# TensorE's instruction order in the token mixers written by hand, and the delta rule's forward substitution moved from VectorE to GpSimd

## The chip, the cores and the metric

The kernel runs on one core of one Trainium2 chip. The metric is device time in microseconds (us) of one execution, lower is better. In the profile the core's engines are PE (TensorE, matrix products), PEld (its weight loads, which overlap PE), DVE (VectorE), ACT (ScalarE), POOL (GpSimd) and SP (SyncE, which issues most transfers).

## The reference, cut to what matters

Two layers over 256 tokens of width 1024. Each layer is a gated feed-forward half step and a layer norm, three token mixers on the same input with gates and one output projection, a norm, a second feed-forward half step and a norm. The change is in the mixers.

```python
def hybrid_layer(x, mem_n, ...):
    h = layer_norm(DEEPNORM_ALPHA * x + 0.5 * swiglu(x, ffn1_w_gu, ffn1_w_down), ln_g[0], ln_b[0])
    (dn_q, dn_k, dn_v, dn_b, dn_a, dn_z, sw_q, sw_k, sw_v, xa_q, gates) = jnp.split(h @ w_in, split_idx, axis=-1)
    o_dn = deltanet_branch(dn_q, dn_k, dn_v, dn_b, dn_a, dn_z, dn_conv_w, ...)
    o_sw = sliding_window_attention(sw_q, sw_k, sw_v, swa_sinks)
    o_xa = memory_cross_attention(xa_q, mem_n, w_mem_kv)
    branches = jnp.stack([o_dn, o_sw, o_xa], axis=2)
    gates = jax.nn.sigmoid(gates.reshape(B_, S_, N_BRANCH, D))
    merged = jnp.sum(gates * jnp.einsum('bsnc,ncd->bsnd', branches, w_branch), axis=2)
    h = layer_norm(DEEPNORM_ALPHA * h + merged @ w_out, ln_g[1], ln_b[1])
    return layer_norm(DEEPNORM_ALPHA * h + 0.5 * swiglu(h, ffn2_w_gu, ffn2_w_down), ln_g[2], ln_b[2])
```

In the DeltaNet branch, keys, queries and values pass a causal convolution of four taps, and each chunk needs a unit triangular system solved:

```python
    a = jnp.where(strict, jnp.einsum('bhncd,bhnsd->bhncs', k_beta, k) * decay, 0.0)
    t_mat = a + jnp.eye(C, dtype=f32)
    sol = lax.linalg.triangular_solve(t_mat, rhs, left_side=True, lower=True, unit_diagonal=True)
```

## The kernel before, in words

**Products.** Every large matrix product takes fp32 operands split into a high and a low part and is done as three passes (high by high, high by low, low by high). Weights come in units of 128x1024 fp32 (512 KB). For each, SP issues the transfer into `raw`, ACT casts the high part (`whi`, L116), DVE subtracts it to leave the low part (`wlo`, L117), and PE multiplies. `projB` (L135 to L137) makes transposed results 256 wide, `projA` with `mm3` (L121 to L123) makes rows of 512. PSUM has three pools: `acc` with four buffers, `at` with two (attention) and `sm` with two (small steps).

**Stages of the mixers.** They take 222 to 482 us of the span in the first layer and 886 to 1149 in the second. First come the projections of z, the gate inputs and the sliding window's values, then three convolutions (k, q, v), the cross-attention's queries (`xq`) and the window's keys and queries (`sq_`). Beside them the DeltaNet is prepared: `tok` turns k, v and q, the decay g is made by a chain of short DVE steps, and the products of keys with keys and queries, times the decay, end up in `AK` (L534 and L535 on PE, L538 on DVE).

**The inverse.** Each triangular system, of 128 rows here, is inverted in blocks. The 16x16 diagonal blocks are gathered by a mask and a sum (L543, L544), written to DRAM on POOL's queue (L546, tile `dr`) and read back spread over 128 partitions (L550, tiles `w2` and `w3`). Fifteen steps of substitution follow, each a product (L576) and a sum (L577) on DVE, 128 partitions by 8x15 elements at first and 8x1 at the end. L581 widens the result to blocks of 32, L583 transposes it, and small products on PE (L597 to L643) double the blocks to 64 and 128, with copies on ACT and POOL between.

**The rest.** The cross-attention (L690 to L713) makes scores, a softmax on DVE and ACT, transposes of the probabilities on PE (L708) and values (L713); the sliding window does the same (L734 to L758). For each branch, gates of 16 units and a branch projection of four units follow, then the output projection.

**What sets the order.** A scheduler orders each engine's queue by the program's order and priorities. Weight transfers and splits get a higher priority. PE's order in the mixers is the scheduler's as well; the program lists all the DeltaNet, then both attentions, then the gates, and the scheduler fills gaps of one with matrix work of another. Each engine runs its queue in order, so an instruction that waits holds up all behind it. Two places restrict it: `together` keeps four small PE instructions adjacent, and the substitution is issued after the last query split:

```python
with tc.issue_after(last_q):
    for j in range(15):
        n = 15 - j
        nc.vector.tensor_tensor(pr16[:, :, 0:n], ab[j // 8][:, j % 8, :, j + 1:16], ...)
        nc.vector.tensor_tensor(y16[:, :, j + 1:16], y16[:, :, j + 1:16], pr16[:, :, 0:n], op=ALU.add)
```

Of the kernel before, what the change touches and what calls it, by code (L numbers as in the profile page):

```python
# [38 lines left out]
def tile_trunk(ctx, tc, x, xT, mem, wst, lnp, memln, cvw, rows, cst, out):  # L39
# [78 lines left out]

    def mm3(o, l, r, first, last, skip=False):
        (lh, ll), (rh, rl) = l, r  # L120
        nc.tensor.matmul(o, lh, rh, start=first, stop=False, skip_group_check=skip)  # L121
        nc.tensor.matmul(o, lh, rl, start=False, stop=False, skip_group_check=skip)  # L122
        nc.tensor.matmul(o, ll, rh, start=False, stop=last, skip_group_check=skip)  # L123

    def projB(xt, nt, kpu, behind=None):
        banks = [acc().rearrange("p (t s) -> p t s", t=2) for _ in range((nt + 1) // 2)]
        for uu in range(KD // kpu):
            hi, lo = unit(behind=behind)
            for kk in range(kpu):
                k = uu * kpu + kk  # L130
                for t in range(nt):
                    c = (kk * nt + t) * P
                    o = banks[t // 2][:, t % 2, :]
                    lastt = t % 2 == 1 or t == nt - 1
                    nc.tensor.matmul(o, hi[:, c:c + P], xt[0](k), start=(k == 0 and t % 2 == 0), stop=False, skip_group_check=True)  # L135
                    nc.tensor.matmul(o, hi[:, c:c + P], xt[1](k), start=False, stop=False, skip_group_check=True)  # L136
                    nc.tensor.matmul(o, lo[:, c:c + P], xt[0](k), start=False, stop=(k == KD - 1 and lastt), skip_group_check=True)  # L137
        return banks

    def projA(xt, w, kpu, nk, outs, tail=0, dsts=(), lead=0, after=None, behind=None, held=()):  # L140
# [23 lines left out]
        for tb in range(2):  # L164
            run(range(lead), tb, range(len(outs[tb])))
        for uu in range(lead, nu - tail):
            for tb in range(2):
                run([uu], tb, range(len(outs[tb])))
# [28 lines left out]
    def to_T(put, tb, src, q):  # L197

        ps = sm()
        for j in range(4):  # L200
            k = q * 4 + j
            nc.tensor.transpose(ps[:, j * P:(j + 1) * P], src[:, k * P:(k + 1) * P], ident)  # L202
# [193 lines left out]
    def mixers(l, hT, mkT, mv_, post):  # L396
        xt = acc_of(hT)

# [17 lines left out]
        def conv(seg, dst):  # L416
            for i, b in enumerate(projB(xt, 4, 2)):
# [7 lines left out]
                silu[:] = [nc.scalar.activation(dst[:, 2 * i:2 * i + 2, :], yc, AF.Silu).ins]  # L425

        kT = T(pu, [P, 4, S], "u0")
        conv(1, kT)
        qT = T(pu, [P, 4, S], "u1")
        conv(0, qT)  # L430
        vT = T(pu, [P, 4, S], "u8")
        conv(2, vT)

        ssq = T(pu, [P, 2, 2, 4], "ssq")
        ktok = T(pu, [P, 4, P], "u9")
        vin = T(pu, [P, 2, 4, P], "u2")

        def tok(src, tb):
            ps = sm()
            for h in range(4):  # L440
                nc.tensor.transpose(ps[:, h * P:(h + 1) * P], src[:, h, tb * P:(tb + 1) * P], ident)
# [7 lines left out]
        for tb in range(2):  # L449
            ps = tok(kT, tb)  # L450
            sumsq(ps, ssq[:, 0, tb, :])
            if tb == 0:
                nc.scalar.copy(ktok, ps)
        nc.vector.tensor_scalar(ssq[:, 0], ssq[:, 0], RMS_EPS, None, ALU.add)
        rk2 = T(pu, [P, 2, 4], "rk2")
        nc.vector.reciprocal(rk2, ssq[:, 0])
        kn = T(pu, [P, 2, 4], "kn")
        rsqrt(kn, ssq[:, 0], T(pu, [P, 2, 4], "knt"))
        nc.vector.tensor_tensor(kn, ssq[:, 0], kn, op=ALU.mult)
        for tb in range(2):  # L460
            ps = tok(vT, tb)
            nc.vector.tensor_tensor(vin[:, tb], ps, kn[:, tb, :].unsqueeze(2).to_broadcast([P, 4, P]), op=ALU.mult)
        for tb in range(2):
            sumsq(tok(qT, tb), ssq[:, 1, tb, :])
        qeps = T(pu, [P, 2, 4], "qeps")
        nc.vector.tensor_scalar(qeps, ssq[:, 1], RMS_EPS, RMS_EPS * P, ALU.add, ALU.mult)
# [38 lines left out]
        ps = sm()  # L505
        gf = g.rearrange("p t h -> p (t h)")
        nc.tensor.matmul(ps[:, 0:8], tri, gf, start=True, stop=True)
        nc.tensor.matmul(ps[:, 8:16], mlt, gf, start=True, stop=True)
        eg = T(pu, [P, 2, 2, 4], "eg")
        nc.scalar.activation(eg.rearrange("p a t h -> p (a t h)"), ps[:, 0:16], AF.Exp)  # L510
        ks = T(pu, [P, 4], "ks")
        nc.vector.tensor_tensor(ks, cS[:, 0, :], eg[:, 1, 0, :], op=ALU.mult)
        neg1 = T(pu, [P, 4], "neg1")
        nc.vector.tensor_scalar(neg1, eg[:, 0, 1, :], -1.0, None, ALU.mult)
        nc.vector.tensor_tensor(ktok, ktok, ks.unsqueeze(2).to_broadcast([P, 4, P]), op=ALU.mult)
# [4 lines left out]
        for c in range(2):  # L520
            gm = TM[c][:, 0]
            nc.gpsimd.tensor_tensor(gm, over4(mlt), hb(g[:, c, :]), op=ALU.mult)
            ps = sm().rearrange("p (h c) -> p h c", h=4)
            for h in range(4):
                nc.tensor.matmul(ps[:, h, :], gm[:, h, :], tri, start=True, stop=True)
            dt = TM[c][:, 1]
            nc.vector.tensor_tensor(dt, ps, over4(dtm), op=ALU.add)
            nc.scalar.activation(dt, dt, AF.Exp)
            cc = slice(c * P, (c + 1) * P)
            for hh in range(2):  # L530
                ps = sm().rearrange("p (h a c) -> p h a c", h=2, a=2)
                for j in range(2):
                    h = 2 * hh + j
                    nc.tensor.matmul(ps[:, j, 0, :], kT[:, h, cc], kT[:, h, cc], start=True, stop=True)  # L534
                    nc.tensor.matmul(ps[:, j, 1, :], kT[:, h, cc], qT[:, h, cc], start=True, stop=True)  # L535
                for j in range(2):
                    h = 2 * hh + j
                    nc.vector.scalar_tensor_tensor(AK[c][:, h], dt[:, h, :].unsqueeze(1).to_broadcast([P, 2, P]), cS[:, c, h:h + 1], ps[:, j], op0=ALU.mult, op1=ALU.mult)  # L538

        cp = T(p2, [P, 2, 4, 16], "t2", bufs=4)  # L540
        for c in range(2):
            tmp = T(p2, [P, 4, P], "t2", bufs=4)
            nc.vector.tensor_tensor(tmp, AK[c][:, :, 0, :], over4(cs[:, C_NB:C_NB + P]), op=ALU.mult)  # L543
            nc.vector.tensor_reduce(cp[:, c], tmp.rearrange("p h (d i) -> p h i d", i=16), axis=AX.X, op=ALU.add)  # L544
        dr = T(pd, [P, P], "dr")
        nc.gpsimd.dma_start(dr, cp.rearrange("p c h i -> p (c h i)"))  # L546
        blocks = dr.rearrange("(d j) n -> d (j n)", j=16)
        for t in range(2):
            src = blocks[:, t * 1024:(t + 1) * 1024].unsqueeze(1).to_broadcast([8, 16, 1024])
            nc.gpsimd.dma_start(TM[t].rearrange("p a h c -> p (a h c)"), src)  # L550
        qd = [slice(32 * i, 32 * i + 32) for i in range(4)]
        L32 = T(pu, [P, 2, 4, 32], "l32")
        for c in range(2):
            for q in qd:
                nc.gpsimd.tensor_tensor(L32[q, c], AK[c][q, :, 0, q], cs[q, C_LV:C_LV + 32].unsqueeze(1).to_broadcast([32, 4, 32]), op=ALU.mult)
        xq = (T(pu, [P, 4, S], "u4", F32R), T(pu, [P, 4, S], "u6", F32R))
        for i, b in enumerate(projB(xt, 4, 2)):
            split(*(t[:, 2 * i:2 * i + 2, :] for t in xq), b)
        (b,) = projB(xt, 1, 8)
        for kv in range(2):  # L560
            hs = slice(kv * 64, kv * 64 + 64)
            split(swk[0][hs, kv, :], swk[1][hs, kv, :], b[hs, 0, :])
        sq_ = (T(pu, [P, 4, S], "u5", F32R), T(pu, [P, 4, S], "sql", F32R))
        for i, b in enumerate(projB(xt, 4, 2)):
            last_q = split(*(t[:, 2 * i:2 * i + 2, :] for t in sq_), b)

        y16 = T(p2, [P, 8, 16], "t2", bufs=4)
        pr16 = T(p2, [P, 8, 15], "t2", bufs=4)
        i16 = cs[:, C_I16:C_I16 + 16].unsqueeze(1).to_broadcast([P, 8, 16])
        nc.gpsimd.tensor_copy(y16, i16)  # L570
        ab = [TM[c].rearrange("p a h (n i) -> p (a h) n i", i=16) for c in range(2)]

        with tc.issue_after(last_q):
            for j in range(15):
                n = 15 - j
                nc.vector.tensor_tensor(pr16[:, :, 0:n], ab[j // 8][:, j % 8, :, j + 1:16], y16[:, :, j:j + 1].to_broadcast([P, 8, n]), op=ALU.mult)  # L576
                nc.vector.tensor_tensor(y16[:, :, j + 1:16], y16[:, :, j + 1:16], pr16[:, :, 0:n], op=ALU.add)  # L577

        W = T(pu, [P, 1024], "w0")
# [343 lines left out]
```

## Time and profile before

| | |
|---|---|
| median of 3 runs | 1343.81 us (1343.74 to 1349.16) |
| the profiled execution | 1345.88 us, span 1344.1 us |
| PE busy | 1307.0 us, 97% |
| PEld busy | 1193.6 us, 89% |
| DVE busy | 851.9 us, 63% |
| ACT busy | 663.4 us, 49% |
| POOL busy | 50.3 us, 4% |
| granted TensorE clock, mean | 0.993 |

A busy share is an average over stages. What ends TensorE's idle time is read from its waits (engine and line that waits, engine and line it waits for, total us, times, longest) and from the timelines. POOL's spans are rough. The granted clock is 1.0 at full speed.

### The profile page before, as it was taken

What the parts mean: (1) busy time and instruction counts of PE and PEld (TensorE: products, weight loads), DVE (VectorE), ACT (ScalarE), POOL (GpSimd) and SP (SyncE); (2) the same over time, 40 slices, a digit from 0 to 9 for tenths busy, and PEclk for the clock granted to TensorE, in tenths of its full rate; (3) what the DMA queues carried; (4) which work ended last, traced back from release to release, by engine and by line L of the source; (5) the groups of instructions that cost most, each with busy time, mean ns of one, the idle gap of its engine ahead of it and who ended that gap; (6) DMA issues with size and microseconds to landing.
All of it is one profiled execution on the core that took longest, in us unless ns stands there. A gap on an engine that the chain in (4) does not pass through costs nothing.

```text
span 1344.1 us, 22686 instructions
## 1 busy us (share of the span) xinstructions
PE 1307.0 (97%) x9112; PEld 1193.6 (89%) x9112; DVE 851.9 (63%) x1332; ACT 663.4 (49%) x1015; POOL 50.3 (4%) x73
## 2 busy tenths in 40 slices
PE   8999999998999999999999999999979999999997
PEld 7999889997777889998899998999967787899986
DVE  5585466797474766554665554758955758655545
ACT  6545344555664535444454444456456645444441
POOL 0000000111001000000000000010200010000000
PEclk9999999999999999999999999999989999999999
DMA  8867565644245736555675555566352557365553
GB/s 260 271 203 247 187 205 169 207 157 112 80 141 160 238 115 205 179 186 188 219 233 190 177 186 188 185 193 204 126 112 64 172 169 238 125 191 187 180 189 118
DMA packets 68585, 240.39 MB, mean 179 GB/s; under 512 B 8160, under 2 KB 9312, under 8 KB 68480
## 3 DMA queue, kind: packets, MB, share of 16 engines
q1 hardware_dynamic: 66176, 232.53, 53.7%
q0 software_dynamic: 2304, 6.43, 2.1%
q8 instruction: 71, 1.16, 0.4%
q14 instruction: 34, 0.28, 0.1%
HBM read 235.64 MB, written 3.28 MB: 178 GB/s over the span
## 4 chain that ended last, share of the span: by engine, by line
PE 80%; DMA 8%; DVE 7%; ACT 3%; issue 1%; SPq 0%; DVEq 0%; ACTq 0%; POOLq 0%
PE acc L136 14%; PE acc L137 14%; PE acc L135 14%; PE acc L122 9%; PE acc L121 9%; PE acc L123 8%; DMA raw<-in_wst_dram 6%; DVE wlo L117 2%; ACT whi L116 2%; DMA w<-dr 2%; PE at L121 1%; PE at L123 1%; PE at L122 1%; PE sm L202 1%; PE sm L643 1%
## 5 line engine op out<-in xcount | busy, mean ns | idle before, releaser
L117 DVE TENSOR_TENSOR wlo<-raw,whi 128x1024 fp32r<-128x1024 f32 (+2 forms) x403 | 486.1, 1210 | 348.6 <-ACT whi L116 346.5
L116 ACT CAST whi<-raw 128x1024 fp32r<-128x1024 f32 (+2 forms) x403 | 414.7, 1034 | 409.6 <-PE acc L136 112.5
L135 PE MATMUL acc<-hThi,whi 128*128 128x256 f32 x1616 | 458.4, 284 | 0.0
L137 PE MATMUL acc<-hThi,wlo 128*128 128x256 f32 x1616 | 457.8, 283 | 0.0
L136 PE MATMUL acc<-hTlo,whi 128*128 128x256 f32 x1616 | 457.4, 283 | 0.0
L135 PEld LDWEIGHTS acc<-hThi,whi 128*128 128x128 f32 x1616 | 310.1, 192 | 0.0
L136 PEld LDWEIGHTS acc<-hTlo,whi 128*128 128x128 f32 x1616 | 310.1, 192 | 0.0
L137 PEld LDWEIGHTS acc<-hThi,wlo 128*128 128x128 f32 x1616 | 309.9, 192 | 0.0
L122 PE MATMUL acc<-wlo,u 128*128 128x512 f32 (+1 forms) x400 | 148.7, 372 | 0.0
L121 PE MATMUL acc<-whi,u 128*128 128x512 f32 (+1 forms) x400 | 148.5, 371 | 0.0
L123 PE MATMUL acc<-whi,u 128*128 128x512 f32 (+1 forms) x400 | 147.2, 370 | 0.0
L121 PE MATMUL acc<-whi,hThi 128*128 128x512 f32 (+1 forms) x272 | 104.6, 385 | 4.9 <-ACT whi L116 4.9
L122 PE MATMUL acc<-wlo,hThi 128*128 128x512 f32 (+1 forms) x272 | 104.5, 384 | 0.0
L123 PE MATMUL acc<-whi,hTlo 128*128 128x512 f32 (+1 forms) x272 | 103.4, 380 | 0.0
L121 PEld LDWEIGHTS acc<-whi,u 128*128 128x128 f32 x400 | 75.4, 188 | 14.1 <-DVE t L309 0.8
L122 PEld LDWEIGHTS acc<-wlo,u 128*128 128x128 f32 x400 | 75.4, 188 | 12.5
L123 PEld LDWEIGHTS acc<-whi,u 128*128 128x128 f32 x400 | 74.9, 188 | 12.9
L116 ACT CAST u<-t 128x256 fp32r<-128x256 f32 x80 | 32.5, 406 | 99.2 <-DVE t L309 99.2
L121 PEld LDWEIGHTS acc<-whi,hThi 128*128 128x128 f32 x272 | 52.4, 193 | 13.2 <-ACT whi L116 4.9
L122 PEld LDWEIGHTS acc<-wlo,hThi 128*128 128x128 f32 x272 | 52.3, 192 | 9.9 <-issue 1.6
L123 PEld LDWEIGHTS acc<-whi,hTlo 128*128 128x128 f32 x272 | 52.3, 192 | 7.9
L117 DVE TENSOR_TENSOR u<-t,u 128x256 fp32r<-128x256 f32 x80 | 34.0, 425 | 32.6 <-ACT u L116 32.6
(310 smaller groups left out, 1487.1 us busy)
## 6 DMA issues: line engine op xcount, KB each, us to landing
raw<-in_wst_dram SPq DMA_DIRECT2D x409, 512.0 KB, 3.6
raw<-in_wst_dram SPq DMA_DIRECT2D x16, 324.0 KB, 3.0
gB<-in_lnp_dram SPq DMA_DIRECT2D x6, 512.0 KB, 6.2
bB<-in_lnp_dram SPq DMA_DIRECT2D x6, 512.0 KB, 6.1
mdr<-w POOLq DMA_DIRECT2D x4, 512.0 KB, 8.4
w<-dr POOLq DMA_DIRECT2D x4, 512.0 KB, 10.7
w<-mdr POOLq DMA_DIRECT2D x4, 512.0 KB, 5.0
t<-in_xT_dram SPq DMA_DIRECT2D x4, 256.0 KB, 5.0
```

What stands on the lines that cost most here:

```text
L116: nc.scalar.copy(hi, src)
L117: return nc.vector.tensor_tensor(lo, src, hi.bitcast(F32), op=ALU.subtract).ins
L121: nc.tensor.matmul(o, lh, rh, start=first, stop=False, skip_group_check=skip)
L122: nc.tensor.matmul(o, lh, rl, start=False, stop=False, skip_group_check=skip)
L123: nc.tensor.matmul(o, ll, rh, start=False, stop=last, skip_group_check=skip)
L135: nc.tensor.matmul(o, hi[:, c:c + P], xt[0](k), start=(k == 0 and t % 2 == 0), stop=False, skip_group_check=True)
L136: nc.tensor.matmul(o, hi[:, c:c + P], xt[1](k), start=False, stop=False, skip_group_check=True)
L137: nc.tensor.matmul(o, lo[:, c:c + P], xt[0](k), start=False, stop=(k == KD - 1 and lastt), skip_group_check=True)
L202: nc.tensor.transpose(ps[:, j * P:(j + 1) * P], src[:, k * P:(k + 1) * P], ident)
L643: together(lambda h: nc.tensor.matmul(ps[:, h, :], *f(h), start=True, stop=True))
```

## The change: what it does

Inside the mixers every PE instruction is now kept in program order, and the program is written in the order wanted. `weave` runs a generator that yields after each unit of weights (`halves`, `gates`) or each block of 512 columns (`branch`), and calls small steps between them. The convolutions and query projections are done in two halves of 256 columns, four blocks of k per unit, with the weights laid out to match; `together` is no longer used there. The substitution, in `inverses`, runs on GpSimd and has no `issue_after`.

```diff
+    pinned = [False]
+    def pe(ins):
+        return tc.keep_in_program_order(ins) if pinned[0] else ins
+    def matmul(*a, **k):
+        return pe(nc.tensor.matmul(*a, **k))
...
+    def weave(work, steps):
+        for n, _ in enumerate(work, 1):
+            for f in steps.get(n, ()):
+                f()
...
+    def halves(xt, use):
+        for i in range(2):
+            (b,) = yield from projB_parts(xt, 2, 4)
+            use(i, b)
...
     def mixers(l, hT, mkT, mv_, post):
         xt = acc_of(hT)
+        pinned[0] = True
...
-        with tc.issue_after(last_q):
-            for j in range(15):
-                n = 15 - j
-                nc.vector.tensor_tensor(pr16[:, :, 0:n], ...)
-                nc.vector.tensor_tensor(y16[:, :, j + 1:16], ...)
+            for j in range(15):
+                n = 15 - j
+                nc.gpsimd.tensor_tensor(pr16[:, :, 0:n], ...)
+                nc.gpsimd.tensor_tensor(y16[:, :, j + 1:16], ...)
-        nc.vector.tensor_tensor(Y32.rearrange("p c h (d i) -> p (c h) d i", d=2), ...)
-        nc.vector.transpose(W[:, 512:768], W[:, 768:1024])
+            nc.gpsimd.tensor_tensor(Y32.rearrange("p c h (d i) -> p (c h) d i", d=2), ...)
...
+        weave(halves(xt, use_xq), {3: [tok_v]})
...
+        decay()
+        weave(halves(xt, use_sq), {
+            1: [lambda: spread(0)],
+            2: [lambda: spread(1), lambda: x_scores(0)],
+            3: [lambda: products(0, 0), lambda: products(0, 1)],
+            4: [lambda: products(1, 0), lambda: products(1, 1), inverses]})
...
+        stages = [doubling(c) for c in range(2)]
+        def double():
+            for d in stages:
+                next(d)
+        def begin_inverse():
+            nc.vector.transpose(W[:, 512:768], W[:, 768:1024])
+            double()
...
+        weave(gates(0), {
+            1: [lambda: x_scores(1)],
+            2: [lambda: x_turn(0)],
+            3: [lambda: x_values(0)],
+            4: [lambda: x_turn(1)],
+            5: [lambda: x_values(1)],
+            6: [lambda: w_scores(0, 0)],
+            7: [lambda: w_scores(0, 1)]})
+        weave(branch(0, oX), {
+            1: [lambda: w_turn(0, 0)],
...
+        weave(gates(1), {
+            1: [lambda: w_scores(1, 1), begin_inverse],
+            2: [double],
+            3: [double],
+            4: [double, lambda: w_turn(1, 0)],
+            5: [double],
+            6: [double, lambda: w_turn(1, 1)],
+            7: [double, lambda: w_values(1)],
+            8: [rec_v0]})
+        weave(branch(1, oS), {
+            1: [rec_s1],
...
+        weave(gates(2), {
+            1: [rec_o0],
+            4: [lambda: finish_turn(1)],
+            5: [lambda: finish_turn(0)]})
```

`x_scores`, `x_turn` and `x_values` are the cross-attention's scores with softmax, transposes and values of one block of 128 tokens; `w_scores`, `w_turn` and `w_values` those of the sliding window. `rec_*` are the recurrence between the two chunks, `finish` and `finish_turn` its normalisation and transposes. The line numbers shift: L121 to L123 become L126 to L128, L708 becomes L129, L543 and L544 become L694 and L695, L546 and L550 become L697 and L701, L555 becomes L704, L576, L577 and L581 become L713 to L715, and L583 becomes L807. Each kernel issues 512-KB weight units in the same number.

Three places of the first layer follow; the second has the same. In VectorE's queue before, where the substitution begins (`t2` are its tiles, `w2` the spread blocks, `mx` the softmax maxima of the cross-attention):

```order
L699 RECIPROCAL sums_561_3775<-sums_561_3775 128x4
L576 TENSOR_TENSOR t2_520_3466<-w2_468_3106,t2_519_3465 128x120
L694 TENSOR_REDUCE mx_565_3804<-at_567_3806 128x2
L577 TENSOR_TENSOR t2_519_3465<-t2_519_3465,t2_520_3466 128x8x15
L695 TENSOR_SCALAR mx_565_3804<-mx_565_3804 128x2
```

and after, at the same place (`w0` holds what L715 writes, `u7` is the low part of the cross-attention's output, `wlo_585` and `wlo_588` belong to branch(0)):

```order
L117 TENSOR_TENSOR wlo_574_3758<-raw_572_3756,whi_573_3757 128x1024
L607 RECIPROCAL sums_537_3557<-sums_537_3557 128x4
L117 TENSOR_TENSOR wlo_582_3803<-raw_580_3801,whi_581_3802 128x1024
L807 STREAM_TRANSPOSE w0_473_3097<-w0_473_3097 128x256
L117 TENSOR_TENSOR u7_550_3635<-at_551_3636,u6_549_3634 128x4x128
L117 TENSOR_TENSOR wlo_585_3823<-raw_583_3821,whi_584_3822 128x1024
L117 TENSOR_TENSOR wlo_588_3829<-raw_586_3827,whi_587_3828 128x1024
```

The thirty steps have left this queue, and the transpose of their result stands where they stood, ahead of the split of the cross-attention's values.

In GpSimd's queue before, from the last products to the merge of the branches:

```order
L555 TENSOR_TENSOR l32_482_3165<-u13_471_3109,cs_87 32x128 x4
L570 COPY t2_519_3465<-cs_87 128x128
L546 DMA dr_481_3161<-t2_478_3154 128x128
L550 DMA w2_468_3106<-dr_481_3161 128x1x1024
L550 DMA w3_469_3107<-dr_481_3161 128x1x1024
L627 COPY w1_522_3501<-w0_521_3498 32x4x32 x8
L782 TENSOR_TENSOR u4_614_4048<-u4_614_4048,gt_662_4284 128x512 x2
```

and after, the first and the last of the steps shown:

```order
L709 COPY t2_526_3495<-cs_87 128x128
L697 DMA dr_525_3483<-t2_522_3476 128x128
L701 DMA w2_464_3086<-dr_525_3483 128x1x1024
L701 DMA w3_465_3087<-dr_525_3483 128x1x1024
L713 TENSOR_TENSOR t2_527_3496<-w2_464_3086,t2_526_3495 128x120
L714 TENSOR_TENSOR t2_526_3495<-t2_526_3495,t2_527_3496 128x8x15
...
L714 TENSOR_TENSOR t2_526_3495<-t2_526_3495,t2_527_3496 128x8
L715 TENSOR_TENSOR w0_473_3097<-t2_526_3495,cs_87 128x256
L785 COPY w1_474_3098<-w0_473_3097 32x4x32 x8
```

The thirty steps and the widening stand between the transfers and the copies of the doubling.

In TensorE's queue before, around the cross-attention's transposes (`at` its PSUM tiles, `whi_630` a unit of the gates):

```order
L708 MATMUL at_572_3836<-cs_87,pp_559_3773 128x128 x4
L121 MATMUL acc_618_4052<-whi_630_4109,hThi_312_2097 128x512
...
L708 MATMUL at_573_3842<-cs_87,pp_559_3773 128x128 x4
L713 MATMUL at_574_3848<-pt_571_3835,u11_342_2330 128x128
L121 MATMUL acc_619_4053<-whi_630_4109,hThi_312_2097 128x512
```

and after, in gates(0):

```order
L126 MATMUL at_551_3636<-pt_543_3603,u11_342_2330 128x128 x8
L126 MATMUL acc_530_3535<-whi_553_3648,hThi_312_2097 128x512
...
L129 MATMUL at_556_3668<-cs_87,pp_535_3555 128x128 x4
L129 MATMUL at_557_3674<-cs_87,pp_535_3555 128x128 x4
L126 MATMUL acc_558_3680<-whi_561_3683,hThi_312_2097 128x512
```

The values of one block, a whole unit of the gates, the transposes of the next block and a next unit now follow one another in fixed order; before, pieces of units stood among the small steps.

More of the change, by code (lines that the diff above doesn't have):

```diff
@@ L527, in mixers, with products @@
             nc.vector.tensor_tensor(dt, ps, over4(dtm), op=ALU.add)
             nc.scalar.activation(dt, dt, AF.Exp)
+        def products(c, hh):
             cc = slice(c * P, (c + 1) * P)
[L530 to L538, printed above, removed]
@@ new lines, in finish_turn, with rec_v0, rec_s1 @@
+        def finish_turn(c):
+            if not oT:
+                oT.extend(T(pu, [P, 4, S], tag, F32R) for tag in ("u8", "u9"))
+            ps = sm().rearrange("p (h c) -> p h c", h=4)
+            for h in range(4):
+                transpose(ps[:, h, :], fin[c][:, h, :], ident)
+            split(oT[0][:, :, c * P:(c + 1) * P], oT[1][:, :, c * P:(c + 1) * P], ps)
+        def rec_v0():
+            nc.scalar.copy(V0, heads(lambda h: (Y[:, 0, h, :], vin[:, 0, h, :])))
+        def rec_s1():
+            nc.scalar.copy(S1, heads(lambda h: (ktok[:, h, :], V0[:, h, :])))
@@ L776, in merge, with branch @@
+                for tb in range(2):
+                    nc.scalar.activation(gt[tb][:, js], outs[tb], AF.Tanh, scale=0.5)
+                yield
+        def branch(n, o):
+            us = [unit() for _ in range(4)]
+            if not mg:
+                mg.extend(T(pu, [P, D], f"u{4 + tb}") for tb in range(2))
+            gt = gts[n]
+            for tb in range(2):
+                ts = slice(tb * P, (tb + 1) * P)
                 for j in range(2):
                     js = slice(j * 512, (j + 1) * 512)
-                    dst = mg[tb] if n == 0 else gt[tb]
```

523 lines of the change are left out of this document (289 added, 234 removed).

## The prediction

> **What bounds the kernel now.** I read the page's busy shares and chain first, then windows over the mixers, then TensorE's waits, then the timelines of the engines it waits for.
>
> ```profile
> PE 1307.0 (97%) x9112; PEld 1193.6 (89%) x9112; DVE 851.9 (63%) x1332; ACT 663.4 (49%) x1015; POOL 50.3 (4%) x73
> PE 80%; DMA 8%; DVE 7%; ACT 3%; issue 1%; SPq 0%; DVEq 0%; ACTq 0%; POOLq 0%
> ...
> 236.00:307.00 71.00, 70.16 (x584) 69.43 (x583) 61.22 (x120) 40.01 (x60) 10.13 (x10) 1.00 0.55 171
> 307.00:360.00 53.00, 46.81 (x447) 37.73 (x446) 28.07 (x69) 31.17 (x78) 5.92 (x15) 0.97 0.40 101
> 971.00:1027.00 56.00, 48.36 (x449) 39.24 (x449) 28.65 (x72) 31.53 (x79) 6.09 (x15) 0.91 0.41 96
> ```
>
> TensorE is busy 97% of the span and carries 80% of the chain; no reordering makes its 1307 us smaller. Only its idle time is to be had. A window's columns are its length, then busy us of PE, PEld, DVE, ACT and POOL, the granted clock, the DMA share and GB/s. The convolutions and queries (236 to 307) leave TensorE 0.8 us; the stretch behind them, where the DeltaNet inverse begins, leaves 6.2 in the first layer and 7.6 in the second. These are TensorE's waits in the mixers (total us, times, longest), its own queue first, then its weight loads:
>
> ```profile
> PE at L708 <- DVE t L577: 13.4, 2, 7.6
> PE at L752 <- ACT pp L749: 1.9, 2, 1.1
> PE sm L202 <- DVE u L782: 1.7, 2, 1.0
> PE sm L534 <- DVE w L527: 1.0, 2, 0.5
> PE sm L663 <- DVE t L660: 0.6, 2, 0.3
> PE sm L507 <- DVE g L504: 0.4, 2, 0.2
> ...
> PEld at L752 <- ACT pp L749: 4.5, 6, 1.5
> PEld at L758 <- ACT pt L753: 2.0, 6, 0.4
> PEld sm L616 <- ACT w L612: 1.5, 4, 0.4
> PEld sm L633 <- ACT w L623: 1.5, 4, 0.4
> ```
>
> The first is the large one: a transpose of the cross-attention (L708) stands behind a VectorE step of the substitution (L577), with which it has nothing to do. The timelines show why (start, length, engine, instruction, idle before and what ended it):
>
> ```profile
> 303.61 1.66 DVE L538 SCALAR_TENSOR_TENSOR u<-w,cS,sm 128x256 f32<-128x256 f32 x4
> 308.28 1.05 DVE L544 TENSOR_REDUCE t<-t 128x64 f32<-128x512 f32 x1
> 322.30 0.28 DVE L576 TENSOR_TENSOR t<-w,t 128x120 f32<-128x120 f32 x1 [7.52 <-DMA w<-dr]
> 988.29 0.28 DVE L576 TENSOR_TENSOR t<-w,t 128x120 f32<-128x120 f32 x1 [9.35 <-DMA w<-dr]
> ...
> 305.36 3.25 POOL L555 TENSOR_TENSOR l<-u,cs 32x128 f32<-32x128 f32 x4 [1.30 <-DVE u L538]
> 308.67 0.29 POOL L570 COPY t<-cs 128x128 f32<-128x128 f32 x1
> 309.63 0.60 POOL L546 DMA_DIRECT2D dr<-t  x1 [0.67 <-DVE t L544]
> 973.79 0.61 POOL L546 DMA_DIRECT2D dr<-t  x1 [0.67 <-DVE t L544]
> ...
> 324.56 1.12 PE L708 MATMUL at<-cs,pp 128*128 128x128 f32 x4 [5.76 <-DVE t L577]
> ```
>
> The coefficients go through DRAM (L546, then L550): 12.67 us from 309.63 to 322.30, 14.50 from 973.79 to 988.29. The first substitution step blocks VectorE's queue for 7.52 and 9.35 us, and the softmax work behind it holds up TensorE.
>
> **The change, part by part.** First, the substitution leaves VectorE. Its 30 steps and the widening step (L576, L577, L581) become L713 to L715 on GpSimd. But VectorE still needs the result: the transpose at L807 reads what L715 writes. In the changed VectorE order L807 stands directly ahead of the split (L117) of x_values(0), whose operand is at_551, and of the splits for branch(0). TensorE's x_turn(1) writes at_556 and at_557; with two "at" buffers, at_557 takes that of at_551 and waits for that split. So the block stays; only what it waits for becomes the transfer plus the whole chain.
>
> ```profile
> L576 DVE TENSOR_TENSOR t<-w,t 128x120 f32<-128x120 f32 (+14 forms) x30 | 6.8, 225 | 17.6 <-DMA w<-dr 16.9
> L782 DVE TENSOR_TENSOR u<-u,gt 128x512 f32<-128x512 f32 x8 | 5.5, 687 | 0.1
> L581 DVE TENSOR_TENSOR w<-t,cs 128x256 f32<-128x256 f32 x2 | 0.9, 426 | 0.1
> L583 DVE STREAM_TRANSPOSE w<-w 128x256 f32<-128x256 f32 x2 | 0.9, 436 | 0.0
> ...
> L555 POOL TENSOR_TENSOR l<-u,cs 32x128 f32<-32x128 f32 x16 | 10.8, 675 | 9.9 <-DVE u L538 9.1
> L782 POOL TENSOR_TENSOR u<-u,gt 128x512 f32<-128x512 f32 x8 | 10.3, 1291 | 140.7 <-DVE gt L779 140.7
> ...
> L117 DVE TENSOR_TENSOR u<-at,u 128x512 fp32r<-128x512 f32 x4 | 2.8, 688 | 2.8 <-ACT u L116 2.8
> ```
>
> One instruction, L782, runs on both engines in one shape: 1291 ns on POOL, 687 on DVE, 1.88 to 1. A step has 225 ns on DVE, so I take 423 ns on POOL: 30 make 12.7 us, and L715, from 426 ns, 0.8: 13.5 per layer. No row has these shapes on POOL. The lower end is its copy of 128x128, the tile that the steps work on, 0.29 us (row at 308.67): 8.8 + 0.8, or 3.9 less. The upper is L555, the same operation at the size of the largest steps, 675 ns: 20.3 + 1.3, or 8.1 more. I stay between, at the scaled value, because the steps shrink to an eighth and L555 ran beside VectorE work, while here VectorE stands still.
>
> Now the stall, from the end of TensorE's last products step. VectorE's last products end some 2.0 later (two of 0.42, the row at 303.61 over 4, and a weight split of 1.24 among them). POOL's four L704 and the copy take 3.25 + 0.29, and the transfer is issued at 5.7 (L544's work on VectorE, now L695, is over earlier). It lands at 18.4 or 20.2; the chain ends at 31.9 or 33.7; L807 (0.44), the split (0.69) and a little for starting make 33.1 or 34.9. TensorE gets there sooner:
>
> ```profile
> 317.27 0.39 PE L121 MATMUL acc<-whi,hThi 128*128 128x512 f32 x1
> ...
> 318.41 0.39 PE L123 MATMUL acc<-whi,hTlo 128*128 128x512 f32 x1
> 329.07 1.80 PE L713 MATMUL at<-pt,u 128*128 128x128 f32 x14
> ```
>
> From 317.27 to 318.41 are five steps of 0.228; four units of gates(0) are 48 of them, 10.9. The small ones start every 0.12 (1.80 less the tail, over 13). Twelve of x_scores(1), eight of x_turn(0), sixteen passes of x_values(0) and four transposes make 4.8. TensorE reaches the wait at 15.7 and stands for 17.4 and 19.2: **36.6 us**, bounds 28.8 (36.6 - 2 x 3.9) and 52.8 (36.6 + 2 x 8.1). Behind the waiting transposes queue all later units, since the order is now fixed; before, matrix work could be put around them.
>
> Were a step's time on POOL in proportion to its elements, L782's row would give 1291 / 512 = 2.5 ns each, 0.16 us for the 64 of a mean step, 4.8 for the thirty and 0.6 for L715: 8.1 less a layer, and 1358. The L555 row is against it: 0.675 at 128 elements, where this gives 0.32, so there is a cost per instruction. The Trainium skill, "GPSIMD Engine Reference", section 3.1, has about 2.6 cycles per element for two-input elementwise work there and keeps VectorE as the rule for it; at its 1.2 GHz that is an estimated 0.14 us a step, and the forecast would be 1357 by it.
>
> Second, the pinned order adds later waits. Rows for their size:
>
> ```profile
> L117 DVE TENSOR_TENSOR wlo<-raw,whi 128x1024 fp32r<-128x1024 f32 x63 | 77.6, 1237 | 36.8 <-ACT whi L116 36.2
> L734 DVE SCALAR_TENSOR_TENSOR pp<-at,cs 128x512 f32<-128x512 f32 x6 | 4.1, 680 | 7.0 <-PE at L123 7.0
> L740 DVE TENSOR_REDUCE mx<-pp 128x4 f32<-128x1024 f32 x2 | 2.4, 1210 | 0.0
> ```
>
> Per layer, from walking the queues by hand, each an estimate: decay waits some 1.5, since g's short VectorE steps end late; the third doubling stage 3.2, its VectorE work standing behind four splits (1.24 each), six L734 and two L740, 11.5 us in all; the fourth 2.3, its copies behind an ACT cast that waits for TensorE to free a buffer; finish_turn 4.7, behind the normalisation's chain. That is 11.7; some overlap, so I take 10, **20 us** for both layers. The bounds are 0, as the same stages wait next to nothing before, and 24, all of them in full. Queued behind each is the whole pinned stream.
>
> Third, what the fixed order saves. Gone are the old waits: 13.4 + 1.9 + 1.7 + 1.0 + 0.6 + 0.4 = 19.0, and of the weight loads what exceeds them: 2.6 (L752, 4.5 against 1.9) + 2.0 + 1.5 + 1.5 = 7.6. Together **26.6**, bounds 19 (the loads' gaps stay) and 34 (as much again as the loads' part).
>
> At no cost: weights laid out in 256-wide halves, with equal bytes, unit size, matmuls and SP transfers, hidden since TensorE is the bound from 236 to 307 (without that cover each unit costs its split, 1.24 on DVE against 2.7 on TensorE, still hidden); 62 fewer steps on DVE, which is not the bound; on POOL the eight copies and the merge sums move behind the chain, where TensorE needs them only after L807.
>
> Last, the clock after a stall:
>
> ```profile
> 324.50:328.00 3.50, 3.44 (x13) 2.91 (x14) 3.29 (x10) 2.44 (x8) 0.00 (x0) 0.60 0.27 55
> 990.50:994.00 3.50, 3.45 (x10) 2.80 (x11) 3.29 (x10) 2.33 (x6) 0.00 (x0) 0.50 0.24 59
> 994.00:998.00 4.00, 4.00 (x24) 3.74 (x23) 3.59 (x16) 2.79 (x6) 0.00 (x0) 0.71 0.63 215
> ```
>
> After 5.8 us of idling it was 0.60 for 3.5 us, after 7.6 us 0.50 and then 0.71: 1.4 and 2.9 us lost. I take the same loss after a longer stall, so 0 more; were it in proportion to the idle time, 4.3 x 36.6 / 13.4 - 4.3 = 7.5 more, 1381. The Trainium skill, "TensorE: Matmul & The Clock Gate", Part 1, has full speed return after about 3.4 us of work however long the idling; by that the first holds, and the trace's slow stretches of 3.5 to 7.5 us agree roughly.
>
> Sum: 36.6 + 20 - 26.6 = +30.0. The profiled execution took 1345.9 (span 1344.1), 2.1 over the median 1343.8; 1375.9 becomes **1374**.
>
> **Rivals.** (1) The later waits do not come, because the stall lets VectorE and ScalarE catch up; the splits' row, with 36.8 us in which VectorE had nothing else to do before them, speaks for it, the order of its queue against: 1374 - 20 = 1354. (2) POOL takes L555's time a step: 1374 + 16 = 1390. (3) Faster: the transfer and chain end before TensorE arrives, so L807 never blocks. That is decided where transfer plus chain fall under 15.7 - 5.7 - 1.2 = 8.8 us; then 20 - 26.6 gives 1337. The transfer alone has 12.67, and only a much shorter one would do. (4) Nothing measurable: the block exists but at its lower end, the later waits are absent: 28.8 - 26.6 = +2, or 34 saved, -5; about 1341 to 1346. (5) POOL's steps cost by their elements alone, as worked out above from L782: 1358. The section of the Trainium skill named there would have it so.
>
> **Chances.** My forecast 0.54, (1) 0.16, (5) 0.04, (2) 0.14, (3) 0.06, (4) 0.06. The range, 1352 to 1396, leaves out (3), (4) and the joint upper bounds. The forecast's own is 1362 to 1384. Half a per cent, 6.7 us, is about what this kernel's measurement can tell: (3) is faster, (4) the same, the rest, 0.88, slower.
>
> **What would show it.** In the profile after: two waits of TensorE at L129 of 17 to 20 us, released through VectorE's L117 or by L807; before them an idle VectorE at L807 that POOL's L715 ends; L713 and L714 near 0.42 us; L708's old wait for L577 gone; waits of some us at the doubling stages. No such wait, or TensorE idle elsewhere in the mixers, makes the prediction wrong; a chain of 20 us makes it too low.

## The result, and the profile after

The changed kernel takes 1381.57 us (median of 4, 1377.25 to 1384.15) against 1343.78 us for the kernel before: the ratio is 1.0274, interval 1.0231 to 1.0318. It is 37.8 us slower; 30 were forecast, and the time lies inside the range. These are the busy shares and the chain of the page after:

```profile
PE 1309.1 (95%) x9112; PEld 1199.5 (87%) x9112; DVE 837.8 (61%) x1270; ACT 660.1 (48%) x1015; POOL 72.5 (5%) x135
...
PE 81%; DVE 6%; DMA 4%; issue 3%; ACT 2%; POOL 2%; SPq 0%; DVEq 0%; POOLq 0%; ACTq 0%
```

TensorE does the same 9112 products in 2.1 us more than before. The span of 1382.4 leaves it 73.3 us idle; before it was 1344.1 - 1307.0 = 37.1. So 36.2 of the 38.3 us between the two profiled executions are idle time, and the windows over the stretch of the inverse show where most of it lies (length, busy us of PE, PEld, DVE, ACT and POOL, clock, DMA share, GB/s):

```profile
236.00:307.00 71.00, 69.93 (x587) 69.75 (x586) 61.62 (x123) 43.77 (x72) 7.23 (x5) 1.00 0.55 173
307.00:360.00 53.00, 34.95 (x186) 29.56 (x186) 21.41 (x35) 18.70 (x40) 16.83 (x43) 0.84 0.37 99
```

The stage before it is unchanged, but in the second window TensorE is idle for 18.1 us, where it was 6.2. Its list of waits names what it waited for:

```profile
PE at L129 <- DVE u L117: 30.7, 2, 15.5
PE sm L129 <- DVE t L831: 11.3, 4, 3.5
PE sm L126 <- ACT w L768: 5.2, 2, 2.6
PE at L129 <- ACT pp L606: 5.2, 4, 2.3
PE acc L126 <- ACT whi L116: 5.1, 1, 5.1
PE sm L129 <- DVE h L279: 3.9, 3, 2.0
PE sm L126 <- DVE g L545: 2.1, 2, 1.1
PE acc L126 <- DVE w L117: 1.6, 2, 0.9
```

The first row is the wait that was forecast. Three timelines of the first layer follow it back from TensorE over VectorE to GpSimd:

```profile
326.73 0.60 PE L129 MATMUL at<-cs,pp 128*128 128x128 f32 x4
342.80 1.11 PE L129 MATMUL at<-cs,pp 128*128 128x128 f32 x4 [15.47 <-DVE u L117]
...
341.73 0.45 DVE L807 STREAM_TRANSPOSE w<-w 128x256 f32<-128x256 f32 x1 [17.01 <-POOL w L715]
342.09 0.65 DVE L117 TENSOR_TENSOR u<-at,u 128x512 fp32r<-128x512 f32 x1
...
314.76 0.60 POOL L697 DMA_DIRECT2D dr<-t  x1
329.25 0.40 POOL L713 TENSOR_TENSOR t<-w,t 128x120 f32<-128x120 f32 x1 [8.94 <-issue]
329.72 0.42 POOL L714 TENSOR_TENSOR t<-t,t 128x120 f32<-128x120 f32 x1
332.09 0.36 POOL L713 TENSOR_TENSOR t<-w,t 128x96 f32<-128x96 f32 x1
340.67 0.22 POOL L714 TENSOR_TENSOR t<-t,t 128x8 f32<-128x8 f32 x1
340.96 0.73 POOL L715 TENSOR_TENSOR w<-t,cs 128x256 f32<-128x256 f32 x1
```

TensorE had done the first four transposes of x_turn(1) at 327.3 (326.73 + 0.60) and had its next operands, but no buffer. VectorE stood at L807 for 17.0 us with the split that would have freed it next in its queue. GpSimd's chain ran from 329.25 to 341.69; L807 ended at 342.18, and TensorE went on at 342.80, behind that split.

### The profile page after: what moved, and what is told of

Same layout as the page of the kernel before. It is cut to its first block, busy times and chain, and to the rows that moved or that the text cites. A ratio compares the mean times of both kernels' runs of the same rounds, so it can differ in the third digit from the quotient of the medians.

```text
span 1382.4 us, 22694 instructions
## 1 busy us (share of the span) xinstructions
PE 1309.1 (95%) x9112; PEld 1199.5 (87%) x9112; DVE 837.8 (61%) x1270; ACT 660.1 (48%) x1015; POOL 72.5 (5%) x135
## 4 chain that ended last, share of the span: by engine, by line
PE 81%; DVE 6%; DMA 4%; issue 3%; ACT 2%; POOL 2%; SPq 0%; DVEq 0%; POOLq 0%; ACTq 0%
PE acc L126 71%; PE at L126 4%; DMA raw<-in_wst_dram 4%; DVE wlo L117 2%; PE sm L126 2%; PE sm L129 1%; ACT whi L116 1%; DVE u L117 1%; POOL t L714 1%; PE acc L318 1%; POOL t L713 1%; POOL l L704 1%; PE acc L315 1%; PE acc L316 1%; PE at L129 1%
## 5 line engine op out<-in xcount | busy, mean ns | idle before, releaser
L117 DVE TENSOR_TENSOR wlo<-raw,whi 128x1024 fp32r<-128x1024 f32 (+2 forms) x403 | 485.2, 1208 | 388.3 <-ACT whi L116 385.6
L126 PE MATMUL acc<-hThi,whi 128*128 128x256 f32 x1616 | 458.9, 284 | 0.0
L126 PE MATMUL acc<-hTlo,whi 128*128 128x256 f32 x1616 | 457.3, 283 | 0.0
L126 PE MATMUL acc<-hThi,wlo 128*128 128x256 f32 x1616 | 457.3, 283 | 0.0
L126 PEld LDWEIGHTS acc<-hTlo,whi 128*128 128x128 f32 x1616 | 310.1, 192 | 0.0
L126 PEld LDWEIGHTS acc<-hThi,whi 128*128 128x128 f32 x1616 | 310.1, 192 | 0.0
L126 PEld LDWEIGHTS acc<-hThi,wlo 128*128 128x128 f32 x1616 | 310.0, 192 | 0.0
L126 PE MATMUL acc<-whi,u 128*128 128x512 f32 (+1 forms) x800 | 246.3, 372 | 0.0
L126 PEld LDWEIGHTS acc<-whi,u 128*128 128x128 f32 x800 | 149.7, 188 | 28.5 <-issue 1.6
L126 PE MATMUL acc<-wlo,u 128*128 128x512 f32 (+1 forms) x400 | 148.4, 371 | 0.0
L126 PE MATMUL acc<-whi,hThi 128*128 128x512 f32 (+1 forms) x272 | 110.0, 405 | 5.1 <-ACT whi L116 5.1
L126 PE MATMUL acc<-wlo,hThi 128*128 128x512 f32 (+1 forms) x272 | 106.5, 391 | 0.0
L126 PE MATMUL acc<-whi,hTlo 128*128 128x512 f32 (+1 forms) x272 | 105.9, 389 | 0.0
L126 PEld LDWEIGHTS acc<-wlo,u 128*128 128x128 f32 x400 | 75.4, 189 | 12.2
L126 PEld LDWEIGHTS acc<-whi,hThi 128*128 128x128 f32 x272 | 54.8, 202 | 15.7 <-ACT whi L116 5.1
L126 PEld LDWEIGHTS acc<-whi,hTlo 128*128 128x128 f32 x272 | 54.1, 199 | 9.7
L126 PEld LDWEIGHTS acc<-wlo,hThi 128*128 128x128 f32 x272 | 54.5, 200 | 8.9 <-DVE wlo L117 0.8
L117 DVE TENSOR_TENSOR u<-t,u 128x256 fp32r<-128x256 f32 x80 | 34.0, 425 | 32.6 <-ACT u L116 32.6
L129 PE MATMUL at<-cs,pp 128*128 128x128 f32 x80 | 13.3, 302 | 35.9 <-DVE u L117 30.7
L129 PEld LDWEIGHTS at<-cs,pp 128*128 128x128 f32 x80 | 9.7, 150 | 38.7 <-DVE u L117 31.2
```

The lines of the kernel that those rows point to most:

```text
L117: return nc.vector.tensor_tensor(lo, src, hi.bitcast(F32), op=ALU.subtract).ins
L126: return pe(nc.tensor.matmul(*a, **k))
L129: return pe(nc.tensor.transpose(*a))
```

## The experiments

All times are medians, ratios are against the kernel before on the same chip, with a 95% interval. "E1" and so on name the runs.

**E1: the one transpose later.** L807 is issued behind the second merge of branch(0).

```diff
-                    nc.vector.scalar_tensor_tensor(dst[:, js], gt[tb][:, js], 1.0, ps, op0=ALU.add, op1=ALU.mult)
+                    merges.append(nc.vector.scalar_tensor_tensor(dst[:, js], gt[tb][:, js], 1.0, ps, op0=ALU.add, op1=ALU.mult).ins)
...
         def begin_inverse():
-            nc.vector.transpose(W[:, 512:768], W[:, 768:1024])
+            with tc.issue_after(merges[1]):
+                nc.vector.transpose(W[:, 512:768], W[:, 768:1024])
             double()
```

> The changed kernel with one instruction put elsewhere in VectorE's queue: the transpose L807 is issued behind the second merge of branch(0) instead of ahead of the split of x_values(0). Substitution stays on GpSimd. Theory (L807 holds VectorE's queue while GpSimd's chain runs, and TensorE's pinned stream waits for the split behind it): both waits of 15.5 and 15.3 us at L129 go, with some 2.5 us of clock loss each, and the inverse still starts in time, since TensorE asks for it some 30 us later: 1381.6 - 30.7 - 5 = 1346, 1340 to 1352. Rival (the pinned order itself is what costs, or the GpSimd chain is needed that early by the doubling): the idle time reappears at the first doubling stage and the time stays at 1370 or above.

Measured: 1350.01 us, ratio 1.0028 (1.0007 to 1.0049). Against the kernel before on its own chip 4.3 us are left of the 37.8; the place of one instruction undoes the rest. In its list of waits the row of 30.7 is gone and the others stand as they were:

```profile
PE sm L129 <- DVE t L832: 11.8, 4, 3.5
PE sm L126 <- ACT w L768: 5.2, 2, 2.6
PE at L129 <- ACT pp L606: 4.9, 3, 2.3
```

The first doubling stage starts at 361.17 without a wait, while GpSimd's chain is done at 345.9:

```profile
345.14 0.74 POOL L715 TENSOR_TENSOR w<-t,cs 128x256 f32<-128x256 f32 x1
...
361.17 1.51 PE L126 MATMUL sm<-w,l 32*32 32x32 f32 x64
```

**E8: a longer chain, once it is hidden.** E1 with each product step on GpSimd done twice, 45 instructions for 30.

```diff
-                nc.gpsimd.tensor_tensor(pr16[:, :, 0:n], ...)
+                for _ in range(2):
+                    nc.gpsimd.tensor_tensor(pr16[:, :, 0:n], ...)
```

> E1 with each product step on GpSimd done twice, the same result: 15 more steps a layer, some 6 to 9 us more chain, which then ends at about 352 to 355 us in the first layer, while TensorE asks for it at 361. Theory (once L807 is out of the way, the chain's length is covered): as E1, 1350, 1346 to 1356. Rival (the chain's length always shows): 1350 + 12 to 18 = 1362 or above.

Measured: 1346.19 us, ratio 1.0018 (0.9999 to 1.0037). The chain ends at 351.2 instead of 345.9 in its trace, and it costs nothing. GpSimd's length matters only through what waits for it.

**E4: a longer chain in the changed kernel.** There the product step is done three times.

```diff
-                nc.gpsimd.tensor_tensor(pr16[:, :, 0:n], ...)
+                for _ in range(3):
+                    nc.gpsimd.tensor_tensor(pr16[:, :, 0:n], ...)
```

> The changed kernel with each product step of the substitution done three times on GpSimd, the same result: 30 more instructions a layer, at 0.385 us from start to start, so 11.6 us more chain. Theory: the chain ends TensorE's wait, so all of it is exposed: the waits at L129 grow from 15.4 to 27 us each, 1381.6 + 23 = 1405, 1400 to 1409. Rival (the transfer through DRAM or an ACT cast ends the wait, the chain runs beside it): 1382, no change.

Measured: 1390.49 us, ratio 1.0331 (1.0307 to 1.0355): 9 us more, not 23. The edit had changed a second thing. With the longer chain the scheduler set L807 (L808 there) two places further back:

```
L117 TENSOR_TENSOR wlo_582_3833<-raw_580_3831,whi_581_3832 128x1024
L117 TENSOR_TENSOR u7_550_3665<-at_551_3666,u6_549_3664 128x4x128
L117 TENSOR_TENSOR wlo_585_3853<-raw_583_3851,whi_584_3852 128x1024
L808 STREAM_TRANSPOSE w0_473_3097<-w0_473_3097 128x256
L117 TENSOR_TENSOR wlo_588_3859<-raw_586_3857,whi_587_3858 128x1024
```

TensorE could then finish x_turn(1) and ran into the same block some units later, at a wait of 16.9 us:

```profile
PE at L126 <- DVE u L117: 33.9, 2, 16.9
```

So the miss does not speak against the chain: it went from 12.4 to 24.3 us (327.92 to 352.2) and TensorE did more work ahead of the block. As a test of the chain's length alone it is inconclusive; with E8 it says that the place in the queue decides.

**E2: the substitution back on VectorE, order pinned.** In the code of the substitution, `nc.gpsimd` becomes `nc.vector`, nothing else.

> The changed kernel with the thirty steps and the widening back on VectorE, TensorE's order pinned as before. Theory: the queue is still blocked by the transfer, but the chain ahead of the split of x_values(0) is now 16 steps of 0.28 and one weight split instead of the whole chain on GpSimd (12.4 us), so TensorE's wait falls from 15.5 to some 9.4 us a layer: 1369, 1363 to 1375. Rival (GpSimd does not matter, only the pinned order does): 1381 as before. Rival (the hand order is harmless, GpSimd alone costs it): 1350 or below.

Measured: 1367.16 us, ratio 1.0160 (1.0138 to 1.0182), and the wait at L129 is less than half:

```profile
PE at L129 <- DVE u L117: 13.7, 2, 8.6
PE sm L129 <- DVE t L831: 11.3, 4, 3.5
```

That is 17.0 us less waiting for 14.4 us of time: so much of the loss goes with the move to GpSimd. The remaining wait is the same queue held up by the transfer and by VectorE's own steps. In the first layer the transfer landed at 327.22, before TensorE came to its wait at 328.3; what it then waited for, 5.1 us, were sixteen steps and a weight split that stand ahead of the split of x_values(0).

**E6: the substitution on VectorE, behind the block.** E1's edit, and the thirty steps issued behind the split of x_values(1).

```diff
+        def substitute():
+            y16, pr16, ab = late
+            with tc.issue_after(xsplit[1]):
+                for j in range(15):
+                    n = 15 - j
+                    nc.vector.tensor_tensor(pr16[:, :, 0:n], ...)
+                    nc.vector.tensor_tensor(y16[:, :, j + 1:16], ...)
...
-            5: [lambda: x_values(1)],
+            5: [lambda: x_values(1), substitute],
```

> E1 with the thirty steps and the widening back on VectorE, but issued behind the split of x_values(1), when the transfer has landed, so that they block nothing. Theory (what matters is the place in VectorE's queue, not the engine; VectorE is idle a third of the time): as E1, 1350, 1346 to 1355. Rival (VectorE's 7.5 us more a layer make the weight splits late, which is what GpSimd saves): 1357 or above.

Measured: 1350.47 us, ratio 1.0047 (1.0029 to 1.0065), as E1. Where the steps block nothing, the engine they run on makes no difference that these runs can tell.

**E3: GpSimd alone.** The kernel before, with the substitution on GpSimd and without its `issue_after`.

> The kernel before with one part alone: the thirty steps and the widening on GpSimd, TensorE's order left to the scheduler. Its transpose (L582 there) now stands behind the second block's softmax maxima and one more weight split. Theory: the longer chain (12.4 against 6.7 us) is covered by about 10 us of gate units whose splits are ahead in the queue; a stall of some 5 us a layer remains, about what it was: 1344, 1338 to 1350. Rival (the engine's slowness alone makes the loss): 1355 or above.

Measured: 1386.93 us, ratio 1.0320 (1.0296 to 1.0343), the largest miss of the theory, which had 1344. The rival's number, 1355 or above, came true. Its waits and windows (of 10 us, after the wait):

```profile
PE sm L596 <- DVE w L582: 29.5, 2, 15.4
...
336.00:346.00 10.00, 9.63 (x125) 8.63 (x125) 2.02 (x5) 4.39 (x13) 1.15 (x4) 0.50 0.16 54
346.00:356.00 10.00, 10.00 (x99) 8.05 (x99) 1.29 (x3) 3.92 (x10) 0.81 (x3) 0.50 0.00 0
356.00:366.00 10.00, 10.00 (x80) 8.53 (x79) 2.57 (x6) 2.68 (x9) 0.34 (x2) 0.50 0.01 2
366.00:376.00 10.00, 10.00 (x58) 8.76 (x57) 3.93 (x9) 7.39 (x20) 0.00 (x0) 0.86 0.16 52
```

I had looked at VectorE's queue alone. In TensorE's, the scheduler had put the first doubling product (L596), which needs the chain's result, in the middle of the unit `whi_630`, so TensorE waited for the chain's result itself, with all its gate units behind; in the kernel before that product stands one unit later, in `whi_635`. E3 thus changed the engine and the order at once and does not price GpSimd alone. A second loss came on top: for 30 us after the wait the granted clock stayed at 0.50, though TensorE was all but fully busy. TensorE is busy 1328.3 us in this profile, 21 more than before. The hand order avoids this wait, since it asks for the inverse only in gates(1).

**E7: the pin off.** The changed kernel with `pinned[0] = False`; the program stands in the new order, and TensorE's queue is the scheduler's again.

> The changed kernel with the pin off: TensorE's order is the scheduler's again, but the program is written in the new order, and VectorE's queue has L807 at the same place. Theory (L807's place makes the loss; the pin itself moves few instructions): 1381, 1374 to 1388. Rival (the pin is what keeps TensorE from other work while it waits): 1365 or below.

Measured: 1366.66 us, ratio 1.0176 (1.0156 to 1.0197), 15 us less than the changed kernel. The theory was wrong: the pin costs 15 us, though not where the rival had it. The long wait is even longer, and the small ones have nearly gone:

```profile
PE at L129 <- DVE u L117: 36.2, 2, 18.5
PE sm L129 <- DVE t L831: 2.3, 2, 1.3
PE sm L126 <- DVE g L545: 0.7, 2, 0.4
PE at L129 <- ACT pp L606: 0.6, 2, 0.3
PE acc L126 <- DVE w L117: 0.5, 2, 0.3
```

The small waits are 4.1 us instead of 25.4, the long one has 5.5 more; in all TensorE idles 14.4 us less and is busy 4.2 us less between the two profiled executions. The scheduler slips a few products of a unit in front of a small step that is not ready (a product at 317.34 stands between the two groups of transposes of x_turn(0), where the wait is 0.28 us instead of 2.32); the pin forbids that.

**E5: steps moved by hand.** E1 with the steps that wait put later in the pinned order; the window's turn goes ahead of the fourth doubling stage, which makes that stage later.

```diff
-        decay()
         weave(halves(xt, use_sq), {
-            1: [lambda: spread(0)],
+            1: [decay, lambda: spread(0)],
...
         weave(gates(0), {
             1: [lambda: x_scores(1)],
-            2: [lambda: x_turn(0)],
-            3: [lambda: x_values(0)],
-            4: [lambda: x_turn(1)],
-            5: [lambda: x_values(1)],
-            6: [lambda: w_scores(0, 0)],
-            7: [lambda: w_scores(0, 1)]})
+            3: [lambda: x_turn(0)],
+            4: [lambda: x_values(0)],
+            5: [lambda: x_turn(1)],
+            6: [lambda: x_values(1)],
+            7: [lambda: w_scores(0, 0)],
+            8: [lambda: w_scores(0, 1)]})
...
-            4: [double, lambda: w_turn(1, 0)],
+            4: [lambda: w_turn(1, 0), double],
...
-            4: [lambda: finish_turn(1)],
-            5: [lambda: finish_turn(0)]})
+            5: [lambda: finish_turn(1)],
+            7: [lambda: finish_turn(0)]})
```

> E1 with small steps put at other places of the hand-written order, by the waits that E1's trace still shows (11.8 at finish_turn, 5.2 at the fourth doubling stage, 4.9 at the first cross-attention turn, 2.1 at decay): finish_turn one and two units later, the cross-attention's and window's steps of gates(0) one unit later, decay one unit later, and the window's turn ahead of the fourth doubling stage. Theory (each wait is a step placed too early in a fixed order, and costs its length): 1350.0 - 11.8 - 4.9 - 2.1 - 1.8 = 1329, 1322 to 1337, below the kernel before (1345.8). Rival (the steps that depend on them become late instead): 1342 to 1352.

Measured: 1336.06 us (1329.31 to 1339.64), ratio 0.9934 (0.9908 to 0.9959), faster than the kernel before. The steps moved lost their waits. Of the fourth doubling stage's 5.2 us 3.4 were left, and 3.2 came up at the fifth:

```profile
PE sm L126 <- ACT w L767: 3.4, 2, 1.7
PE sm L126 <- ACT w L774: 3.2, 2, 1.6
...
PE sm L129 <- DVE t L831: 0.4, 1, 0.4
```

**E9, E10 and E11: both losses taken away.** E9 is E1 with the pin off, E10 is E5 with the pin off, E11 is E6 with the pin off; each is one line, `pinned[0] = False`.

> E1 with the pin off: the new order of the program, L807 behind the second merge of branch(0), TensorE's order the scheduler's. Theory (the two losses add: L807's place 30 to 36 us and its clock, the pin's later waits some 15): E7 less its two waits at L129 and their clock, 1366.7 - 36.2 - 5 = 1325, 1319 to 1333, below E5. Rival (without the block the pin costs nothing, since those waits come from the late work alone): as E1, 1344 to 1352.

> E5 with the pin off. Theory: the steps have been moved off their waits by hand, so the scheduler's freedom has only the doubling stages' 6.6 us and the turns' 1.3 left to remove: 1336.1 - 7 = 1329, 1322 to 1336, within 5 us of E9. Rival (moving by hand and freeing the order add in full, 14 us more than E5): 1322 or below.

> E6 with the pin off: substitution on VectorE behind the split of x_values(1), TensorE's order the scheduler's. Theory (once it blocks nothing, the engine of the substitution is worth little): within 5 us of E9, 1318 to 1329. Rival (with TensorE's small waits gone, VectorE's 13 us more come through): 1331 or above.

Measured: E9 1323.39 us, ratio 0.9843 (0.9823 to 0.9863); E10 1321.96, 0.9836 (0.9817 to 0.9855); E11 1327.09, 0.9849 (0.9824 to 0.9873). The three can't be told apart, and each is some 1.5% faster than the kernel before. E10's time lies just under its theory's range and has the rival's number, 14.1 us under E5's median, yet between the two profiled executions it is 8.0 us (spans 1327.8 and 1319.8), near the theory's 7; E5's times lie 10 us apart, so this is not settled. From the span of the changed kernel E1 takes 36.0 us, E7 18.6 and E9 60.8: the two losses add, and the 6.2 us over are about the 5.5 by which the long wait had grown in E7. E11 shows that the gain over the kernel before needs no GpSimd. It comes with the new order of the program and nothing standing in VectorE's queue in front of a late result; which part of that order, the halves or the places, brings it was not separated. This is the page of E9, with its longest wait in the mixers:

```profile
PE 1299.6 (98%) x9112; PEld 1189.9 (90%) x9112; DVE 838.5 (63%) x1270; ACT 659.7 (50%) x1015; POOL 80.0 (6%) x135
...
PE sm L129 <- DVE t L832: 3.2, 2, 1.9
```

## Why the prediction was right, and where its terms were off

- **The block at L807 (forecast 36.6 us, measured 30.7).** The mechanism, the place and the engines are those of the trace, and E1 takes them away. Its parts were off in both directions. A step on GpSimd took 0.31 us (mean of L713 and L714) against 0.423, but with 0.08 between two steps the chain came to 12.4 against 13.5 us. The transfer took 14.5 and 15.9 us (314.76 to 329.25 in the first layer) against 12.7 and 14.5: its second hop (L701) was issued 4.3 us after the first, where L550 was issued 2.4 after L546. What held it is not shown. TensorE arrived 18.5 us after the end of its last products step, not 15.7, since it had lost 2.6 us on the way at the first cross-attention turn, a wait that the sum did not have.
- **The later waits (forecast 20 us, measured 25.4).** E7 confirms the term: with the pin off 21.3 of them go. Of its parts, decay's had 1.05 us a layer for 1.5, the fourth doubling stage 2.6 for 2.3, finish_turn 5.65 for 4.7. The third doubling stage's 3.2 never came, and the first cross-attention turn's 2.6 was not forecast. Nor was one of 0.8 a layer for the split of the merged branches (L117), so the 25.4 lie above the bound of 24. That rival (1), where they would be absent, did not come is the pin's doing.
- **The savings (forecast 26.6 us, measured about 19).** This is the mis-sized step. The waits of TensorE's own queue went as counted, 19.0 us. The 7.6 us of weight loads were no idle time of TensorE: the rows of its own queue explain 28.7 of the 37.1 us idle before and 65.4 of the 73.3 after, which leaves 8.4 and 7.9 for all else. The weight loads overlap the products here, and their gaps must not be added.
- **The clock (forecast no more than before).** TensorE's busy time grew by 2.1 us. The windows behind the first layer's wait of 15.5 us have a clock of 0.50 and 0.68:

```profile
342.00:345.50 3.50, 2.70 (x9) 2.31 (x10) 1.87 (x3) 0.59 (x1) 0.00 (x0) 0.50 0.17 28
345.50:349.00 3.50, 3.50 (x16) 2.89 (x15) 0.00 (x0) 0.48 (x1) 0.00 (x0) 0.68 0.32 122
349.00:352.00 3.00, 3.00 (x21) 2.66 (x20) 1.92 (x2) 1.15 (x2) 0.00 (x0) 1.00 0.06 15
```

  That is close to the 0.50 and 0.71 after 7.6 us before: 2.5 us lost here and 2.8 in the second layer, against 2.9 then, so beyond 7.6 us the loss did not grow with the wait. The Trainium skill ("TensorE: Matmul & The Clock Gate", Part 1) has it so, with some 3.4 us of work to full speed. Here it took 4.8 and 5.6 us until products started every 0.23 us again instead of every 0.43, and in E3 some 30 us of work did not bring it back, which is against the rule. What the term left out is that a short wait can cost too: in the second layer the clock was 0.51 from 1003.0 to 1006.5, behind a wait of 2.3 us, and 1.7 us were lost; behind the same wait in the first layer it stayed at 1.00. The prediction's first premise, that no reordering makes TensorE's 1307 us smaller, failed through the clock as well: the same products took 1299.6 in E9 and 1298.1 in E11, at a mean clock of 0.997 and 0.999 against 0.993.
- **Sum.** 30.7 + 25.4 - 19.0 + 2.1 - 0.9 (what else was idle) = 38.3, as between the two profiled executions. The forecast of 30 took the stall 5.9 us too long; the later waits were 5.4 too short, savings of 7.6 were none and the clock cost 2.1. That the first two nearly cancel is luck, and so is part of the later waits' total, since a forecast part that never came was made up by two that were not forecast.
- **Rivals.** POOL at 0.675 a step (2) and at 0.16 by elements alone (5) both missed: the steps took 0.40 us at 120 elements and 0.22 at 8, so there is a cost per instruction of about 0.2 us. At 64 elements they took 0.31 and 0.32 us. By the figure of 2.6 cycles per element of the Trainium skill ("GPSIMD Engine Reference", section 3.1) it would be an estimated 0.14; for these small tiles the two differ, and the measurement decides. The transfer never came near the 8.8 us at which (3) would have begun. The stall came near the lower end of (4), 28.8, but the later waits were there; by its own terms (4) reached down to 1339, not 1341.

What stays open: why E3's clock stayed at 0.50 for 30 us. The products in that stretch are mostly of 32x32, 64x64 and transposes, but no run separates that from other causes. A doubled chain with the queue's order held was not tried either, since E4's order moved. What sets off the loss of clock behind a wait of 2.3 us in one layer and not in the other is open as well.

## What to carry to other kernels

Moving slow work to an idle engine frees nothing if an instruction that reads its result stays where the work was: look in the order for the first reader on each in-order queue, and at what stands behind it. An order fixed by hand pays every small lateness in full; E9 had the gain of the new order without the pin, and E5 got part of it by moving each step that waits to a later place. When a wait is costed, take it from the bottleneck engine's own queue and not from its loads as well.

## What the runs showed of the hardware that I had not expected

GpSimd's elementwise steps are held up beside one kind of VectorE's steps. In E1, where VectorE works beside the chain, its steps had a mean of 427 and 440 ns instead of 307 and 317. Two rows of E1's timelines show one of them:

```profile
332.29 1.31 DVE L117 TENSOR_TENSOR wlo<-raw,whi 128x1024 fp32r<-128x1024 f32 x1 [2.40 <-ACT whi L116]
...
332.59 1.23 POOL L713 TENSOR_TENSOR t<-w,t 128x96 f32<-128x96 f32 x1
333.89 0.38 POOL L714 TENSOR_TENSOR t<-t,t 128x96 f32<-128x96 f32 x1
```

The step L713 of 96 elements took 0.36 us in the changed kernel and 1.23 here, ending 0.2 us after the weight split that ran beside it, and L714 behind it was back at 0.38. Four steps of this layer's chain are of that kind, 1.11 to 1.23 us long, each ending some 0.2 us after a weight split that ran beside it. Steps beside VectorE's reductions (L654) and its readings of PSUM tiles (L648) kept their length. They make most of the difference between the chain's 16.1 us and 12.4, at no cost, since the chain was hidden. What the two engines share there, no run shows.
